# Parameters in three PSUM tiles, the second store in two halves, and two stores made one, in a batch normalisation that streams 33.6 MB

## Chip, cores, metric

One NeuronCore of a Trainium2 chip; the other cores are idle. The metric is device microseconds (us) of one execution, as a median over runs. The profiler's span is about 1.8 us shorter than the device time (81.7 against 83.5 us).

## Reference

```python
batch, channels, h, w = 32, 128, 32, 32          # x: float32
normalized = (x - running_mean[None, :, None, None]) / np.sqrt(running_var[None, :, None, None] + eps)
scaled = normalized * gamma[None, :, None, None] + beta[None, :, None, None]
return np.maximum(scaled, 0).astype(np.float32)
```

As a table x has 4096 rows (image and channel) of 1024 floats, 4 KB each. The kernel lays 16 consecutive rows into each of 128 partitions, and does this twice: t = 0 and t = 1, the first and the second half. "Row j" of a half is the j-th row of every partition: 128 x 4 KB = 512 KB.

## The kernel before

The parts that the change and the argument touch; cuts are marked with `# ...`.

```python
TILES = ((0, 0, 2), (0, 2, 4), (0, 4, 8), (0, 8, 16), (1, 0, 16))   # (half, first row, end)
LOAD_CUTS = {(1, 8)}
STORE_CUTS = {(0, 1)}
HALVES = {(1, 0), (1, 1)}
# ... all loads are issued by SP, in order: rows 0-1, 2-3, 4-7, 8-15, then 0-7 and 8-15 of half 1
    raw = params.tile([Q, 4, J], F32, name="raw")
    for k, src in enumerate((running_var, gamma, running_mean, beta)):
        nc.scalar.dma_start(out=raw[:, k, :], in_=src.rearrange("(q j) -> q j", j=J))
    # ... rep: a 0/1 matrix that spreads the 8 rows of parameters over 128 partitions
    cols = psum.tile([P, 4, J], F32, name="cols")
    for a, b in ((0, 2), (2, 3), (3, 4)):
        nc.tensor.matmul(cols[:, a:b, :]..., rep..., raw[:, a:b, :]..., start=True, stop=True)
    # ... std_t = sqrt(var + eps) on ACT; on DVE: rstd_t, scale_t, ms_t, bias_t
    with tc.manual_schedule(engines={mybir.EngineType.Activation}):
        for t, a, b, xt in tiles:
            first = a
            for j in range(a, b):
                # ... one activation for row j (two for rows in HALVES): Relu(scale * x + bias), in place
                if j + 1 == b or (t, j + 1) in STORE_CUTS:
                    nc.scalar.dma_start(
                        out=outr[t, :, first : j + 1, :], in_=xt[:, first - a : j + 1 - a, :]
                    )
                    first = j + 1
```

So there are six stores: row 0, row 1, rows 2 to 3, 4 to 7 and 8 to 15 of the first half, and the whole second half. In the profile one packet is the contiguous piece of one partition: rows 0 and 1 go out in 4 KB packets, rows 2 to 3 in 8 KB packets, the whole half in 64 KB packets.

Of the kernel before, what the change touches and what calls it, by code (L numbers as in the profile page):

```python
# [1 line left out]

# [4 lines left out]


F32 = mybir.dt.float32
ACTF = mybir.ActivationFunctionType  # L10



J = 16

TILES = ((0, 0, 2), (0, 2, 4), (0, 4, 8), (0, 8, 16), (1, 0, 16))

LOAD_CUTS = {(1, 8)}
STORE_CUTS = {(0, 1)}

HALVES = {(1, 0), (1, 1)}


@with_exitstack
def kernel(
    ctx: ExitStack,
    tc: tile.TileContext,
    x: bass.AP,
    gamma: bass.AP,
    beta: bass.AP,  # L30
    running_mean: bass.AP,
    running_var: bass.AP,
    eps: bass.AP,
    out: bass.AP,
):
    nc = tc.nc
    B, C, H, W = x.shape
    HW = H * W
    P = nc.NUM_PARTITIONS
    assert C % J == 0 and P % (C // J) == 0 and (B * C) % (P * J) == 0  # L40
    Q = C // J
    T = B * C // (P * J)

    xr = x.rearrange("b c h w -> (b c) (h w)").rearrange("(t p j) w -> t p j w", p=P, j=J)
    outr = out.rearrange("b c h w -> (b c) (h w)").rearrange("(t p j) w -> t p j w", p=P, j=J)

    data = ctx.enter_context(tc.tile_pool(name="data", bufs=1))
    params = ctx.enter_context(tc.tile_pool(name="params", bufs=1))
    psum = ctx.enter_context(tc.tile_pool(name="psum", bufs=1, space=bass.MemoryType.PSUM))

    tiles = []
    for t, a, b in TILES:
        xt = data.tile([P, b - a, HW], F32, name=f"x{t}_{a}")
        cuts = [a] + [j for j in range(a + 1, b) if (t, j) in LOAD_CUTS] + [b]
        for c, d in zip(cuts, cuts[1:]):
            nc.sync.dma_start(out=xt[:, c - a : d - a, :], in_=xr[t, :, c:d, :])  # L56
        tiles.append((t, a, b, xt))



    raw = params.tile([Q, 4, J], F32, name="raw")
    for k, src in enumerate((running_var, gamma, running_mean, beta)):
        nc.scalar.dma_start(out=raw[:, k, :], in_=src.rearrange("(q j) -> q j", j=J))
    eps_t = params.tile([P, 1], F32, name="eps_t")
    nc.vector.memset(eps_t, float(eps))  # L65
    rep = params.tile([Q, P // Q, Q], F32, name="rep")
    nc.gpsimd.memset(rep, 1.0)  # L67
    nc.gpsimd.affine_select(  # L68
        out=rep,
        in_=rep,  # L70
        compare_op=mybir.AluOpType.is_equal,
        fill=0.0,
        base=0,
        pattern=[[0, P // Q], [-1, Q]],
        channel_multiplier=1,
    )
    cols = psum.tile([P, 4, J], F32, name="cols")


    for a, b in ((0, 2), (2, 3), (3, 4)):  # L80
        nc.tensor.matmul(  # L81
            cols[:, a:b, :].rearrange("p k j -> p (k j)"),
            rep.rearrange("q r s -> q (r s)"),
            raw[:, a:b, :].rearrange("q k j -> q (k j)"),
            start=True,
            stop=True,
        )
    std_t = params.tile([P, J], F32, name="std_t")
    nc.scalar.activation(out=std_t, in_=cols[:, 0, :], func=ACTF.Sqrt, bias=eps_t[:, 0:1], scale=1.0)  # L89
    rstd_t = params.tile([P, J], F32, name="rstd_t")  # L90
    nc.vector.reciprocal(out=rstd_t, in_=std_t)  # L91
    scale_t = params.tile([P, J], F32, name="scale_t")
    nc.vector.tensor_mul(out=scale_t, in0=cols[:, 1, :], in1=rstd_t)  # L93
    ms_t = params.tile([P, J], F32, name="ms_t")
    nc.vector.tensor_mul(out=ms_t, in0=cols[:, 2, :], in1=scale_t)  # L95
    bias_t = params.tile([P, J], F32, name="bias_t")
    nc.vector.tensor_sub(out=bias_t, in0=cols[:, 3, :], in1=ms_t)  # L97

    with tc.manual_schedule(engines={mybir.EngineType.Activation}):
        for t, a, b, xt in tiles:  # L100
            first = a
            for j in range(a, b):
                step = HW // 2 if (t, j) in HALVES else HW
                for w in range(0, HW, step):
                    nc.scalar.activation(  # L105
                        out=xt[:, j - a, w : w + step],
                        in_=xt[:, j - a, w : w + step],
                        func=ACTF.Relu,
                        bias=bias_t[:, j : j + 1],
                        scale=scale_t[:, j : j + 1],  # L110
                    )
                if j + 1 == b or (t, j + 1) in STORE_CUTS:
                    nc.scalar.dma_start(
                        out=outr[t, :, first : j + 1, :], in_=xt[:, first - a : j + 1 - a, :]
                    )
                    first = j + 1


# [1 line left out]
_INS = ['x', 'gamma', 'beta', 'running_mean', 'running_var', 'eps']  # L120
_OUTS = [((32, 128, 32, 32), 'float32')]

_NUMBERS = {'eps': 1e-05}


# [26 lines left out]
```

## Time and profile before

| | before |
|---|---|
| device time | 83.57 us median of 6 (83.50 to 83.71) |
| span of the profile | 81.7 us |
| ACT busy | 39.1 us |
| loads (q1) | 48.6% of 81.7 us = 39.7 us per DMA engine |
| stores and parameters (q10) | 47.8% of 81.7 us = 39.1 us per DMA engine |

The two DMA rows are the ones to read. Multiply a queue's share by the span and you have the packet time of that queue on each of the 16 DMA engines (packet time is the time from a packet's start to its end). The prediction works with these two rows and shows the lines. The timeline says when a store is issued (start, duration, engine and line; `x2` would be two issues in one entry):

```profile
9.44 1.24 ACT L105 ACTIVATE x<-x,bias_t,scale_t 128x1024 f32<-128x1024 f32 x1 [1.02 <-DVE bias_t L97]
10.71 0.38 ACTq L113 DMA_DIRECT2D out_dram<-x  x1
...
12.41 0.37 ACTq L113 DMA_DIRECT2D out_dram<-x  x1
...
55.95 0.34 ACTq L113 DMA_DIRECT2D out_dram<-x  x1
```

The waits of SP show that its last two loads are not issued at once; each waits for an earlier transfer with which it shares a semaphore:

```profile
SPq L56 <- DMA raw<-in_running_mean_dram: 4.0, 1, 4.0
SPq L56 <- DMA x<-in_x_dram: 0.9, 1, 0.9
```

### The profile page before, as it was taken

Reading aid. Unit: us, or ns where it says so; the run is one execution under the profiler, and the core shown is the slowest. Engines: PE = TensorE matmul, PEld = TensorE weight load, DVE = VectorE, ACT = ScalarE, POOL = GpSimd, SP = SyncE. Lnnn points to the kernel's source line nnn. Section 1 sums busy time; section 2 is a strip of 40 time slices with the busy share of each in tenths; the row PEclk is TensorE's granted clock in tenths of the full one; section 3 lists DMA queues with packets and bytes.
Section 4 is the critical chain, followed back from the end, with each engine's and each line's share of the span. In section 5 each row is a group of like instructions: output and inputs, shape, how many; then the busy total and the mean of one; then the engine's idle time right before and its main releaser. Section 6 shows DMA issues by size and latency. Waiting matters only on the chain.

```text
span 81.7 us, 128 instructions
## 1 busy us (share of the span) xinstructions
PE 1.7 (2%) x6; PEld 1.5 (2%) x6; DVE 0.8 (1%) x5; ACT 39.1 (48%) x36; POOL 0.8 (1%) x6
## 2 busy tenths in 40 slices
PE   0008000000000000000000000000000000000000
PEld 0007000000000000000000000000000000000000
DVE  0000300000000000000000000000000000000000
ACT  0600477799039999199997199993000000000000
POOL 3000000000000000000000000000000000000000
DMA  2899999989899898969789699996991999998290
GB/s 44 313 422 481 409 481 417 497 369 497 369 385 481 375 491 357 541 293 605 321 373 589 273 489 393 513 497 273 513 770 64 449 513 513 513 513 385 128 513 0
DMA packets 1793, 33.56 MB, mean 411 GB/s; under 512 B 257, under 2 KB 257, under 8 KB 513
## 3 DMA queue, kind: packets, MB, share of 16 engines
q1 hardware_dynamic: 864, 16.78, 48.6%
q10 hardware_dynamic: 928, 16.78, 47.8%
q14 instruction: 1, 0.00, 0.0%
HBM read 16.78 MB, written 16.78 MB: 411 GB/s over the span
## 4 chain that ended last, share of the span: by engine, by line
DMA 56%; ACT 10%; issue 2%; SPq 0%
DMA x<-in_x_dram 56%; ACT x L105 10%; SPq L56 0%
## 5 line engine op out<-in xcount | busy, mean ns | idle before, releaser
L105 ACT ACTIVATE x<-x,bias_t,scale_t 128x1024 f32<-128x1024 f32 (+1 forms) x34 | 37.5, 1178 | 10.0 <-DMA x<-in_x_dram 7.7
L89 ACT ACT_TABLE_LOAD x1 | 1.3, 1283 | 2.7 <-issue 2.7
L89 ACT ACTIVATE std_t<-cols,eps_t 128x16 f32<-128x16 f32 x1 | 0.3, 276 | 4.2 <-PE cols L81 4.2
L81 PE MATMUL cols<-raw,rep 8*128 8x16 f32 (+1 forms) x6 | 1.7, 384 | 6.4 <-DMA raw<-in_gamma_dram 6.3
L81 PEld LDWEIGHTS cols<-raw,rep 8*128 8x128 f32 x6 | 1.5, 307 | 6.5 <-issue 6.3
L68 POOL TENSOR_SCALAR_AFFINE_SELECT rep<-rep 8x128 f32<-8x128 f32 x1 | 0.4, 394 | 0.1
L91 DVE RECIPROCAL rstd_t<-std_t 128x16 f32<-128x16 f32 x1 | 0.3, 253 | 7.5 <-ACT std_t L89 7.5
L67 POOL MEMSET rep<- 8x128 f32 x1 | 0.2, 195 | 0.3 <-POOLq L133 0.3
L93 DVE TENSOR_TENSOR scale_t<-cols,rstd_t 128x16 f32<-128x16 f32 x1 | 0.2, 174 | 0.1
L95 DVE TENSOR_TENSOR ms_t<-cols,scale_t 128x16 f32<-128x16 f32 x1 | 0.2, 174 | 0.0
L97 DVE TENSOR_TENSOR bias_t<-cols,ms_t 128x16 f32<-128x16 f32 x1 | 0.2, 174 | 0.0
L133 POOL MEMSET const-bfloat16-1.0<- 128x1 bf16 x1 | 0.1, 108 | 0.0
L133 POOL MEMSET const-float32-0.0<- 128x1 f32 x1 | 0.1, 105 | 0.3 <-issue 0.3
L133 POOL MEMSET const-uint8-127<- 128x1 uint8 x1 | 0.1, 107 | 0.0
L133 POOL MEMSET const-float32-1.0<- 128x1 f32 x1 | 0.1, 105 | 0.0
L65 DVE MEMSET eps_t<- 128x1 f32 x1 | 0.1, 59 | 0.9 <-PEq L133 0.9
## 6 DMA issues: line engine op xcount, KB each, us to landing
x<-in_x_dram SPq DMA_DIRECT2D x3, 4096.0 KB, 38.6
out_dram<-x ACTq DMA_DIRECT2D x1, 4096.0 KB, 28.6
x<-in_x_dram SPq DMA_DIRECT2D x2, 1024.0 KB, 5.8
x<-in_x_dram SPq DMA_DIRECT2D x1, 2048.0 KB, 11.3
out_dram<-x ACTq DMA_DIRECT2D x1, 2048.0 KB
out_dram<-x ACTq DMA_DIRECT2D x2, 512.0 KB, 19.1
out_dram<-x ACTq DMA_DIRECT2D x1, 1024.0 KB
raw<-in_running_var_dram ACTq DMA_DIRECT2D x1, 0.5 KB
```

The costliest lines, as they stand in the source:

```text
L65: nc.vector.memset(eps_t, float(eps))
L67: nc.gpsimd.memset(rep, 1.0)
L68: nc.gpsimd.affine_select(out=rep, in_=rep, compare_op=mybir.AluOpType.is_equal, fill=0.0, base=0, pattern=[[0, P // Q], [-1, Q]], channel ...
L81: nc.tensor.matmul(cols[:, a:b, :].rearrange("p k j -> p (k j)"), rep.rearrange("q r s -> q (r s)"), raw[:, a:b, :].rearrange("q k j -> q ...
L89: nc.scalar.activation(out=std_t, in_=cols[:, 0, :], func=ACTF.Sqrt, bias=eps_t[:, 0:1], scale=1.0)
L91: nc.vector.reciprocal(out=rstd_t, in_=std_t)
L93: nc.vector.tensor_mul(out=scale_t, in0=cols[:, 1, :], in1=rstd_t)
L95: nc.vector.tensor_mul(out=ms_t, in0=cols[:, 2, :], in1=scale_t)
L97: nc.vector.tensor_sub(out=bias_t, in0=cols[:, 3, :], in1=ms_t)
L105: nc.scalar.activation(out=xt[:, j - a, w : w + step], in_=xt[:, j - a, w : w + step], func=ACTF.Relu, bias=bias_t[:, j : j + 1], scale=sc ...
L133: nc = _bacc.Bacc("TRN2", target_bir_lowering=False, num_devices=1)
```

## The change

The intent is to start the stores sooner and to use fewer, larger packets: three PSUM tiles let the square root start when the first pair of parameters is there; row 1 is stored in two halves of 64 partitions; rows 4 to 15 leave in one store of 48 KB packets. One more row of the second half is computed in two activations.

```diff
-TILES = ((0, 0, 2), (0, 2, 4), (0, 4, 8), (0, 8, 16), (1, 0, 16))
+TILES = ((0, 0, 2), (0, 2, 4), (0, 4, 16), (1, 0, 16))
-LOAD_CUTS = {(1, 8)}
+LOAD_CUTS = {(0, 8), (1, 8)}
+TWO_PARTS = {(0, 1)}
-HALVES = {(1, 0), (1, 1)}
+HALVES = {(1, 0), (1, 1), (1, 2)}
-    raw = params.tile([Q, 4, J], F32, name="raw")
+    raw = {}
+    for a, srcs in ((0, (running_var, gamma)), (2, (running_mean,)), (3, (beta,))):
+        raw[a] = params.tile([Q, len(srcs), J], F32, name=f"raw{a}")
 ...
-    cols = psum.tile([P, 4, J], F32, name="cols")
+    cols = []
     for a, b in ((0, 2), (2, 3), (3, 4)):
+        c = psum.tile([P, b - a, J], F32, name=f"cols{a}")
 ...
                 if j + 1 == b or (t, j + 1) in STORE_CUTS:
-                    nc.scalar.dma_start(
-                        out=outr[t, :, first : j + 1, :], in_=xt[:, first - a : j + 1 - a, :]
-                    )
+                    parts = P // 2 if (t, j) in TWO_PARTS else P
+                    for p in range(0, P, parts):
+                        nc.scalar.dma_start(
+                            out=outr[t, p : p + parts, first : j + 1, :],
+                            in_=xt[p : p + parts, first - a : j + 1 - a, :],
+                        )
```

The loads are the same six as before.

More of the change, by code (lines that the diff above doesn't have):

```diff
@@ L57 @@
         tiles.append((t, a, b, xt))
-    raw = params.tile([Q, 4, J], F32, name="raw")
-    for k, src in enumerate((running_var, gamma, running_mean, beta)):
-        nc.scalar.dma_start(out=raw[:, k, :], in_=src.rearrange("(q j) -> q j", j=J))
+    raw = {}
+    for a, srcs in ((0, (running_var, gamma)), (2, (running_mean,)), (3, (beta,))):
+        raw[a] = params.tile([Q, len(srcs), J], F32, name=f"raw{a}")
+        for k, src in enumerate(srcs):
+            nc.scalar.dma_start(out=raw[a][:, k, :], in_=src.rearrange("(q j) -> q j", j=J))
     eps_t = params.tile([P, 1], F32, name="eps_t")
@@ L76 @@
     )
-    cols = psum.tile([P, 4, J], F32, name="cols")
+    cols = []
     for a, b in ((0, 2), (2, 3), (3, 4)):
+        c = psum.tile([P, b - a, J], F32, name=f"cols{a}")
         nc.tensor.matmul(
-            cols[:, a:b, :].rearrange("p k j -> p (k j)"),
+            c.rearrange("p k j -> p (k j)"),
             rep.rearrange("q r s -> q (r s)"),
-            raw[:, a:b, :].rearrange("q k j -> q (k j)"),
+            raw[a].rearrange("q k j -> q (k j)"),
             start=True,
@@ L87 @@
         )
+        cols.append(c)
     std_t = params.tile([P, J], F32, name="std_t")
-    nc.scalar.activation(out=std_t, in_=cols[:, 0, :], func=ACTF.Sqrt, bias=eps_t[:, 0:1], scale=1.0)
+    nc.scalar.activation(
+        out=std_t, in_=cols[0][:, 0, :], func=ACTF.Sqrt, bias=eps_t[:, 0:1], scale=1.0
+    )
     rstd_t = params.tile([P, J], F32, name="rstd_t")
@@ L92 @@
     scale_t = params.tile([P, J], F32, name="scale_t")
-    nc.vector.tensor_mul(out=scale_t, in0=cols[:, 1, :], in1=rstd_t)
+    nc.vector.tensor_mul(out=scale_t, in0=cols[0][:, 1, :], in1=rstd_t)
     ms_t = params.tile([P, J], F32, name="ms_t")
-    nc.vector.tensor_mul(out=ms_t, in0=cols[:, 2, :], in1=scale_t)
+    nc.vector.tensor_mul(out=ms_t, in0=cols[1][:, 0, :], in1=scale_t)
     bias_t = params.tile([P, J], F32, name="bias_t")
-    nc.vector.tensor_sub(out=bias_t, in0=cols[:, 3, :], in1=ms_t)
+    nc.vector.tensor_sub(out=bias_t, in0=cols[2][:, 0, :], in1=ms_t)
     with tc.manual_schedule(engines={mybir.EngineType.Activation}):
@@ L112 @@
                 if j + 1 == b or (t, j + 1) in STORE_CUTS:
-                    nc.scalar.dma_start(
-                        out=outr[t, :, first : j + 1, :], in_=xt[:, first - a : j + 1 - a, :]
-                    )
+                    parts = P // 2 if (t, j) in TWO_PARTS else P
[3 more added lines that the diff above has]
+                            in_=xt[p : p + parts, first - a : j + 1 - a, :],
+                        )
                     first = j + 1
```

## The prediction

> **What bounds the kernel now.** I read the page first, slice by slice. The DMA row is the mean busy share of the 16 DMA engines in tenths, the ACT row that of the only engine that computes on x.
>
> ```profile
> span 81.7 us, 128 instructions
> ...
> ACT  0600477799039999199997199993000000000000
> ...
> DMA  2899999989899898969789699996991999998290
> ```
>
> ACT is finished by slice 27 of 40 (about 56 us) and has holes before that. The DMA row stays at 8 to 9 almost throughout; the low digits near the end are large packets counted in one slice or the next, not rests. The queue list gives the proof: q1 carries the loads, q10 the stores and the four small parameter loads.
>
> ```profile
> q1 hardware_dynamic: 864, 16.78, 48.6%
> q10 hardware_dynamic: 928, 16.78, 47.8%
> HBM read 16.78 MB, written 16.78 MB: 411 GB/s over the span
> ```
>
> 48.6% + 47.8% = 96.4% of 81.7 us is 78.8 us of packet time on every engine. Only 2.9 us of the span are left. The packet records of the trace say where those lie: the first packet starts 1.8 us after the span's start, the last ends at 80.6 us, and the rest is the closing semaphores. Between the two the number of packets in flight is 16 in every microsecond. The view by windows, cut at the landings of the loads (busy time is in the first columns, DMA share and GB/s in the last two), agrees:
>
> ```profile
> 12.00:23.00 11.00, 0.00 (x0) 0.00 (x0) 0.00 (x0) 7.38 (x7) 0.00 (x0) 1.00 0.99 419
> 23.00:34.00 11.00, 0.00 (x0) 0.00 (x0) 0.00 (x0) 9.16 (x8) 0.00 (x0) 1.00 1.00 430
> 34.00:46.40 12.40, 0.00 (x0) 0.00 (x0) 0.00 (x0) 9.71 (x10) 0.00 (x0) 1.00 1.01 433
> 46.40:80.20 33.80, 0.00 (x0) 0.00 (x0) 0.00 (x0) 9.16 (x8) 0.00 (x0) 1.00 1.00 433
> ```
>
> DMA share is 0.99 to 1.01 in every stretch. The 33.80 us after the last load are stores alone, at 433 GB/s. So the kernel is bound by bytes through 16 engines, with no idle time inside. The chain that ended last names ACT and the loads, but it stops at the issue of the last store (55.95 us) and cannot see that this store then queues behind others. The waits of ACT show what the change aims at:
>
> ```profile
> ACT x L105 <- DMA x<-in_x_dram: 7.7, 3, 3.6
> ...
> ACT std_t L89 <- PE cols L81: 4.2, 1, 4.2
> ...
> ACT x L105 <- DVE bias_t L97: 1.0, 1, 1.0
> ```
>
> ACT waits 4.2 us for all of cols before the square root, and 1.0 us for the bias. These waits are on the way to the first store, not on the way to the end, as long as the loads keep the engines full meanwhile.
>
> **What the Trainium skill says.** The page "DMA: Bandwidth & Descriptors", section "Where 436 GB/s comes from", puts the ceiling at 435.2 GB/s; the 433 of the last window agrees, so the store phase has no speed to gain. The same page, "Queues, rings and completion order", says that each engine takes turns between its queues at packet granularity. The packet records agree: until the loads end, each 32 KB load packet (1.22 us) alternates with one store packet, whatever its size (4 KB 0.159 us, 8 KB 0.309 us). The same page, "Rules for kernel authors", on two transfers to disjoint partition halves: "Don't bother — they serialize"; no transfer of 64 partitions is in this trace, so it cannot confirm it. The page "PSUM — Partial Sum Buffer", section "PSUM bank collisions raise a hardware error", asks to guard PSUM by bank, not by address. That fits the trace: std_t needs only the first pair of matmuls but starts at 8.15 us, just after the sixth.
>
> **Part 1, three PSUM tiles.** Same four small transfers, same six matmul passes, same DVE instructions; only the waits move. By the trace gamma lands and PE starts at 6.3 us, the first parameter pair is in PSUM at 6.93 us, the mean at 7.48, beta at 8.11 (each held up by the landing of its parameter). Now: std_t at 8.15, reciprocal 8.45, scale 8.82, ms 9.03, bias 9.23, first ReLU at 9.44. After: std_t at about 7.0, reciprocal 7.3, scale about 7.7, ms about 7.9 (mean is there), bias waits for beta until about 8.15, first ReLU about 8.4. So about 1.05 us sooner, and the first store is issued at about 9.65 in place of 10.71 us. Until then loads alone hold all 16 engines busy (window 2 to 12 us: share 1.00), so a store that starts sooner only takes turns sooner. Gain at the end: 0.0.
>
> **Part 2, row 1 stored in two.** One more issue on ACT's queue (0.34 to 0.38 us each in the trace). The bytes and the 4 KB packets are the same, 8 per engine in all, if each half spreads over all 16 engines. ACT does idle later (3.59 us before rows 8 to 15, 2.27 us before the last eight rows), so 0.4 us there is absorbed. With part 3 the number of stores stays six. Cost: 0.0.
>
> **Part 3, rows 4 to 15 of the first half in one store.** A sum by packet size, per engine, from the packet records: eight packets of 16 KB at 0.611 us and eight of 32 KB at 1.213 us become eight of 48 KB. 64 KB takes 2.418, so doubling 32 KB saves 2 x 1.213 - 2.418 = 0.008 us and doubling 16 KB saves 0.009. Estimate for 48 KB: 0.611 + 1.213 - 0.008 = 1.816 us. Saved: 8 x 0.008 = 0.07 us. That is all the change removes from the bounding engines.
>
> The danger is in when this store is issued: at about 33 us instead of 20.27 for its first third. But the store queue serves in order, and with one store packet per load packet it is busy with rows 0 to 3 for very long: these are 24 packets per engine, and the loads of rows 8 to 15 and of the second half are also 24. In the trace rows 2 and 3 finish only at 46.7 us, when the loads (46.4 us) are just done. So the 16 KB packets that could have started at 20 us started at 46.4 us, and the late store still has 13 us to spare. With part 1 the small stores finish perhaps 1 us sooner, which leaves 12.
>
> **Part 4, row 2 of the second half in two halves.** Two activations of 0.80 us in place of one of 1.23: +0.37 us on ACT, before a hole of 2.27 us. Cost: 0.0.
>
> **The end.** After the loads, the stores of rows 4 to 15 and of the whole second half are left: 14.7 MB, 33.9 us at 433 GB/s. The last store (rows 0 to 15 of the second half) must be issued before the queue runs dry. Now: last load lands at 46.7, eight activations take 9.16 us, issue at 55.95; the store before it ends at 61.2 us. Margin 5 us, less one or two for the way from issue to first packet. After: about 0.2 us more store packets come between the loads, so issue at about 56.2 us, and the 48 KB packets end at about 61. The margin holds.
>
> Sum: 83.55 - 0.07 + 0.0 = 83.48 us.
>
> **Rivals.**
> (a) The earlier start is passed on to the end: 83.55 - 1.05 = 82.5 us. This would need engines that idle for lack of stores. Against it: 16 packets in flight in every microsecond from 2 to 80. I give it 2%.
> (b) A half of 64 partitions is served badly (fewer engines, or two engines pulling from the same part of SBUF). For it: the form is new here. Estimate: if its 8 packets of 0.159 us per engine took twice as long, 1.3 us if it all fell on the sum, 84.8 us; more likely only part, 83.7 to 84.2. About 8%.
> (c) A new wait at the issue of a store. Transfers share a few semaphores, and some wait for an earlier transfer to land before they are issued (SP waits 4.0 us for a parameter in front of a load of x). If the last store came to wait for the store just before it (61 us), the engines would run dry: about 1 us of wait after the last packet and some 1.5 to 3.9 us to the first packet of the new one, 85.5 to 88 us. Against it: there are sixteen transfers before and after, and the last one's partner was the store of row 0, landed long before. 2%.
> (d) The pair of 64-partition stores, or the shifted turns, put the engines out of step so that one ends later. Now the 16 engines end within 0.34 us of each other; a few tenths at most.
>
> **Range and chances.** The three runs before lie within 0.12 us. Below, nothing but 0.07 us and startup scatter (the first 8 KB load packets average 0.344 us against 0.309, so 16 x 0.035 = 0.6 us per engine is the most that luck could give). Above, (b) and (d). Range 83.2 to 83.9 us. Faster by over 2% needs 1.7 us out of 2.9 us of idle span, which the change doesn't touch: 1%. Slower by over 2% needs (c): 2%.
>
> **What would show it.** Right: first ReLU near 8.4 us; q1 and q10 again about 96% together, with the same bytes and some 128 fewer packets; 48 KB packets of about 1.82 us beginning when the loads end, near 46.5 us; the last store issued near 56 us; DMA share 1.00 in each window; the span at 81.6 us. Wrong: a window after 46 us with a share under 0.97 (rival c); 4 KB store packets well over 0.16 us (rival b); or a first packet or last landing that moved by more than 0.3 us.

## The result

| | before | after |
|---|---|---|
| device time, median of 6 | 83.57 us | 83.53 us |
| range | 83.50 to 83.71 | 83.44 to 83.74 |
| span of the profile | 81.7 us | 81.7 us |
| first ReLU / first store issued | 9.44 / 10.71 us | 8.33 / 9.60 us |
| last load has landed / last store issued | 46.7 / 55.95 us | 46.8 / 56.05 us |

The ratio is 0.9996 (95% interval 0.9981 to 1.001). Ratios here are the mean of one kernel's runs over the mean of the other's in the same rounds, so they are not quite the ratios of the medians quoted beside them. Executions over 1.5% slower than the fastest of the same kernel are left out of the means.

The page of the kernel after, the span and the queues:

```profile
span 81.7 us, 129 instructions
...
q1 hardware_dynamic: 864, 16.78, 48.6%
q10 hardware_dynamic: 800, 16.78, 47.7%
```

128 packets fewer on q10, and 0.1% of the span (0.08 us) less packet time. Its windows, cut as the prediction cut those of before:

```profile
12.00:23.00 11.00, 0.00 (x0) 0.00 (x0) 0.00 (x0) 7.00 (x6) 0.00 (x0) 1.00 0.99 418
23.00:34.00 11.00, 0.00 (x0) 0.00 (x0) 0.00 (x0) 9.16 (x8) 0.00 (x0) 1.00 1.00 427
34.00:46.40 12.40, 0.00 (x0) 0.00 (x0) 0.00 (x0) 9.99 (x11) 0.00 (x0) 1.00 1.03 441
46.40:80.20 33.80, 0.00 (x0) 0.00 (x0) 0.00 (x0) 9.16 (x8) 0.00 (x0) 1.00 0.99 430
```

The share (the number before the last) is as full as before. The waits of ACT moved as intended, 4.2 to 2.7 us for PSUM:

```profile
ACT std_t L95 <- PE cols L86: 2.7, 1, 2.7
```

The timeline shows the start 1.1 us sooner and, at 11.30, the two issues of row 1, which take 1.18 us where the one issue took 0.37; the last store is not sooner:

```profile
8.33 1.24 ACT L113 ACTIVATE x<-x,bias_t,scale_t 128x1024 f32<-128x1024 f32 x1 [1.46 <-DVE bias_t L105]
9.60 0.39 ACTq L123 DMA_DIRECT2D out_dram<-x  x1
...
11.30 1.18 ACTq L123 DMA_DIRECT2D out_dram<-x  x2
...
56.05 0.34 ACTq L123 DMA_DIRECT2D out_dram<-x  x1
```

One thing was not foreseen: the semaphores are shared out differently, and the last load is now issued at 12.77 us instead of 8.11, since SP waits for rows 4 to 7 to land:

```profile
SPq L58 <- DMA x<-in_x_dram: 5.0, 1, 5.0
```

It costs nothing, because the data of that load do not move before 34 us in either kernel.

### The profile page after: what moved, and what is told of

The parts are those of the page before. It is cut to its first block, busy times and chain, and to the rows that moved or that the text cites. A ratio compares the mean times of both kernels' runs of the same rounds, so it can differ in the third digit from the quotient of the medians.

```text
span 81.7 us, 129 instructions
## 1 busy us (share of the span) xinstructions
PE 1.8 (2%) x6; PEld 1.5 (2%) x6; DVE 0.8 (1%) x5; ACT 39.3 (48%) x37; POOL 0.8 (1%) x6
## 4 chain that ended last, share of the span: by engine, by line
DMA 55%; ACT 10%; issue 2%; SPq 1%
DMA x<-in_x_dram 55%; ACT x L113 10%; SPq L58 1%
```

## The experiments

All agree with the reference. Each ran beside the kernel before on the same chip. The medians of before in the three sets were 83.54 us (first four runs), 83.55 (next four) and 83.49 (last four).

The first theory was that of the prediction: the engines are always full, only the sum of packet times counts, each part is worth about nothing. The rival was that two effects cancel.

### Undo part 1: one raw tile, one cols tile

```diff
-    raw = {} ...; c = psum.tile([P, b - a, J], ...) per pair
+    raw = params.tile([Q, 4, J], F32, name="raw"); cols = psum.tile([P, 4, J], F32, name="cols")
```

> The changed kernel with part 1 undone: one raw tile and one cols tile again. First theory (engines always full, an earlier first store only takes turns earlier): first ReLU back at about 9.4 us, time 83.5 us, ratio to the kernel before 0.998 to 1.002. Rival (two effects cancel: the earlier start gives about 1 us and another part takes it away): about 84.5 us, ratio about 1.012.

Measured: 83.92 us, ratio 1.0046 (1.0031 to 1.0061). It lies between the two: too slow for the first theory, and not slow enough for the rival.

### Undo part 2: row 1 in one store

```diff
-TWO_PARTS = {(0, 1)}
+TWO_PARTS = set()
```

> The changed kernel with row 1 stored in one transfer of 128 partitions. First theory: nothing at the end, 83.5 us, although ACT starts row 2 about 0.8 us sooner. Rival (the 64-partition pair costs what the earlier start gives): 82.5 us, ratio 0.988.

Measured: 84.34 us, ratio 1.0095 (1.0082 to 1.0109). Both were wrong: without the pair of halves the kernel is slower by 0.8 us, although ACT starts row 2 sooner.

### Undo part 3: rows 4 to 7 and 8 to 15 stored separately

```diff
-STORE_CUTS = {(0, 1)}
+STORE_CUTS = {(0, 1), (0, 8)}
```

> The changed kernel with rows 4 to 7 and 8 to 15 stored separately again, in packets of 16 and 32 KB. First theory: eight packets of 48 KB (1.815 us) become eight of 16 KB (0.611) and eight of 32 KB (1.213), 0.07 us more per engine: 83.6 us, too little to be told from noise. The sum of packet times in the trace should be 0.07 us higher per engine. Rival (the late issue of the joined store costs, hidden by the gain of the earlier start): 82.5 to 83.0 us.

Measured: 83.77 us, ratio 1.003 (1.0015 to 1.0045). The packet records give 14.59 us per engine for rows 4 to 15 instead of 14.52, the 0.07 us of the theory; the rest of the 0.23 us is not in the stores. The interval lies above that of the changed kernel (0.9981 to 1.001), so the difference is not noise alone. Its runs spread from 83.64 to 84.05, and the profiled one was the 84.05.

### All stores in two halves of 64 partitions

```diff
-                    parts = P // 2 if (t, j) in TWO_PARTS else P
+                    parts = P // 2
```

> Every store of x in two transfers of 64 partitions each, also the large ones. First theory (each half spreads over all 16 engines, four packets on each, at the same time per packet): 83.5 us, packets of 64 KB still at 2.418 us. Rival (64 partitions are served by fewer engines, or two engines pull from the same part of SBUF at half the rate): the 33.8 us of stores after the loads take up to twice as long, so anything from 90 to 115 us.

Measured: 116.81 us, ratio 1.398. The rival holds for the large stores. Two windows of this run, both stores alone (the last three numbers are clock, DMA share, GB/s):

```profile
46.80:60.00 13.20, 0.00 (x0) 0.00 (x0) 0.00 (x0) 8.90 (x8) 0.00 (x0) 1.00 1.00 233
60.00:74.00 14.00, 0.00 (x0) 0.00 (x0) 0.00 (x0) 0.00 (x0) 0.00 (x0) 1.00 1.03 229
```

The share is 1.0, and the rate is 233 GB/s where the kernel after has 430. A full DMA row says that packets are in flight, not that they are fast: 64 KB packets took 4.68 us on average here, 2.418 before. The 4 KB packets, which take turns with loads, still took 0.159 us. So the form leaves the packet time as it was where the change uses it, and nearly doubles it for a store that has the engines to itself. Fewer engines are not the reason: 15 to 17 packets were in flight at every microsecond from 47 to 110 us. That two engines pull from the same part of SBUF fits this, but no run shows it.

### The start made 6 and 20 us later

```diff
+    # ... idle_t: an unused tile of 128 x 1024, set to 0 by GpSimd
+        for _ in range(5):        # 16 in the second run
+            nc.scalar.activation(out=idle_t, in_=idle_t, func=ACTF.Relu, ...)
         for t, a, b, xt in tiles:
```

> The changed kernel with five activations on an unused tile in front of the first ReLU, which starts 5.7 us later (5 x 1.13). First theory (the start of the stores has slack, since loads fill the engines and the small stores only take turns): 83.5 us. Rival (the first store's time is passed on to the end): 89 us.

> The same with sixteen unused activations: first ReLU about 18.1 us later, at 26.4. ACT then never waits for a load any more: rows 0 to 15 done at about 47, the last store issued at about 65.9 us in place of 56.05. The loads end about 42.5 us, the store queue runs dry once near 47 (about 2 us) and again before the last store (about 4 us). First theory: the slack is used up and the time grows by about 6 us, to 89.6 us (87 to 92). If the slack were unlimited: 83.5; if every microsecond counted: 101.6.

Measured: 84.23 us (ratio 1.0081) and 92.20 us (1.1031). An unused activation takes 1.27 us (20.34 / 16), not 1.13; the rows of x take 1.145 (9.16 / 8). That each waits for the one before it, since all work in place on one tile, would explain this, but is not shown. The first ReLU was 6.5 and 20.4 us later. Of 6.5 us, 0.7 us reached the end, so the slack is real but not free. Of 20.4 us, 8.7 us did. The windows of the second run show where: the engines ran dry twice, once for 3.3 us and once for 4.1 us.

```profile
46.90:50.20 3.30, 0.00 (x0) 0.00 (x0) 0.00 (x0) 2.88 (x4) 0.00 (x0) 1.00 0.01 5
...
65.60:69.70 4.10, 0.00 (x0) 0.00 (x0) 0.00 (x0) 3.31 (x3) 0.00 (x0) 1.00 0.00 0
```

The last store left at 68.94 us; I had expected 65.9 and 89.6 us in all. The longer activations explain most of the miss.

### Rows 0 to 3 in one store of 16 KB packets

```diff
-TILES = ((0, 0, 2), (0, 2, 4), (0, 4, 16), (1, 0, 16))
+TILES = ((0, 0, 4), (0, 4, 16), (1, 0, 16))
-LOAD_CUTS = {(0, 8), (1, 8)};  STORE_CUTS = {(0, 1)};  TWO_PARTS = {(0, 1)}
+LOAD_CUTS = {(0, 2), (0, 8), (1, 8)};  STORE_CUTS = set();  TWO_PARTS = set()
```

> Rows 0 to 3 of the first half stored in one transfer, 16 KB packets, 8 per engine in place of 24 small ones. Same bytes, fewer and larger packets, so the sum of packet times is slightly lower. First theory (one store packet per load packet, whatever its size): the store of rows 4 to 15, issued near 34 us, then takes turns with the last loads, eight times 1.82 + 1.22 us, so the last load lands at about 60 us in place of 46.8, the last store is issued about 70 us, the engines run dry for about 10 us, time about 94 us (90 to 96). Rival (only the sum of packet times counts, the order of the stores is free): 83.5 us.

Measured: 93.79 us; of four runs one took 99.65 us and is left out of the ratio, 1.1212. As expected from turns of one packet each, large store packets now stood between the last loads. ACT's waits and a window of this run:

```profile
ACT x L113 <- DMA x<-in_x_dram: 23.6, 3, 12.7
```

```profile
62.50:71.00 8.50, 0.00 (x0) 0.00 (x0) 0.00 (x0) 7.68 (x7) 0.00 (x0) 1.00 0.00 0
```

ACT waited 12.7 us for the last load, and the DMA engines then stood still for 8.5 us for want of a store. Fewer and larger packets cost 10 us. The 24 small store packets per engine in the two kernels are what lets the 24 large load packets through.

### All stores from row 2 on in 8 KB packets

```diff
-STORE_CUTS = {(0, 1)}
+STORE_CUTS = {(0, 1)} | {(t, j) for t in (0, 1) for j in range(2, 16, 2)}
```

> All stores from row 2 on in pieces of two rows, 8 KB packets. First theory (the time is fixed cost plus the sum of packet times): 15 pieces x 8 x 0.309 + 16 x 0.159 = 39.6 us of store packets per engine in place of 38.9, so 0.75 us more: 84.3 us, unless a piece has to wait for an earlier one to land and the queue runs dry. Rival (the size of packets does not matter): 83.5 us.

Measured: 84.80 us, ratio 1.0138 (1.0107 to 1.017). The packet records give 39.63 us for the stores, as worked out (0.75 us more). The other 0.5 us are not in the stores: in the profiled run the loads took 0.2 us longer than in the kernel after (39.9 against 39.7 us per engine), and the engines' last packets ended 1.16 us apart instead of 0.43.

### Reading the turns

Four of these runs (part 1 undone, part 2 undone, 6 us later, 8 KB packets) were 0.4 to 0.8 us slower than the sum of the stores allows. The packet records show it. They do not name the engine, so I chained them: each packet follows the one that ended when it started, in sixteen chains. Where several packets end within nanoseconds of each other a chain can cross to another engine, so the counts below are surer than any single chain. Below is the commonest chain of each kernel, from the first 32 KB load on; L is a load packet of 32 KB, 4 and 8 are store packets of 4 and 8 KB, and | is where the large stores begin.

```
before      LL4L4L4L4L4L4L44LL4L4L4L4L4L4L44LL8L8L8L8L8L8L88|
after       L4L4L4L4L4L4L4L4L4L4L4L4LL4L4L44LL8L8L8L8L8L8L88|
undo part 1 LL4L4L4L4L4L4L44LL4L4L4L4LL4L44L4LL8L8L8L8L8L888|
undo part 2 L4L4L4L4L4L4L4L4L4L4L4L4L4L4L4L4L8L8L8L8L8L8L8L8|
6 us later  LLLLLLL4L44L4L4L4L4L4LL4L44L4LL4L4L4L4LL88888888|
```

Two loads in a row (LL) are a turn that the store queue missed; mostly this happens where one store ends and the next begins. Part 1 lets the stores enter one load sooner. Part 2 adds a boundary, and with it one missed turn. Together they leave the stores where they were: in the kernels before and after, every engine has just two small packets left when its last load ends. Undo one part and it is three, or one.

That was the second theory: **parts 1 and 2 offset each other through the phase of the turns**, and a phase other than that of before costs 0.3 to 0.8 us. Four runs tested it, and all four came out within the ranges given in advance.

### Part 1 alone and part 2 alone, on the kernel before

The edits are the hunks for raw and cols, and the hunk with `TWO_PARTS`, of the diff above.

> The kernel before with part 1 alone (three raw and three cols tiles). New theory (parts 1 and 2 offset each other: what counts is how many small store packets each engine has left when its last load ends; 2 on every engine in the kernels before and after): first ReLU about 8.4 us, first store packet one load packet sooner, so 1 packet left, engines out of step, about 84.2 us (83.8 to 84.5). First theory (engines are full, nothing counts but the sum of packets): 83.55 us.

> The kernel before with part 2 alone (row 1 stored in two halves). New theory: the additional boundary between two stores costs the store queue one turn, so 3 small packets are left at the end of the loads, the last load packet is longer (about 1.5 us in place of 1.22) and the time about 83.9 us (83.7 to 84.1). First theory: 83.55 us.

Measured: 84.16 us (ratio 1.0078, 1.0065 to 1.0091) and 83.98 us (1.0065, 1.0052 to 1.0078), with one packet left (none to two) and three (two to four). Each part alone makes the kernel slower; both together do not.

### One unused activation, with and without the halves

```diff
+        for _ in range(1):
+            nc.scalar.activation(out=idle_t, in_=idle_t, func=ACTF.Relu, ...)
         for t, a, b, xt in tiles:
```

The first run has it in the kernel with part 2 undone, the second in the changed kernel.

> The changed kernel with row 1 in one store (84.34 us when it ran alone) and one unused activation in front of the first ReLU, which moves the first store 1.13 us later, back to where the kernel before has it. New theory (only the phase of the turns counts, not the form with 64 partitions): 2 packets left on every engine, 83.5 us (83.4 to 83.7), faster than without the additional work. Rival (the 64-partition form itself brings the gain): still 84.3 us. Rival (additional work on ACT costs something): 84.3 or more.

> The changed kernel with one unused activation in front of the first ReLU, the first store 1.13 us later. New theory: one turn later, 3 packets left, like the run with part 1 undone: 83.9 us (83.7 to 84.1). First theory: 83.5 us.

Measured: 83.57 us median (six runs: four from 83.49 to 83.59, one 83.80, one 84.45; ratio 1.0035, 1.0003 to 1.0067) and 83.83 us (1.0047, 1.0035 to 1.0059). **The same additional work, 1.1 us before the first store, takes 0.77 us off one kernel (84.34 to 83.57) and adds 0.30 us to the other (83.53 to 83.83).** These are medians from different sets; by the ratios to the kernel before it is about 0.5 us off (1.0095 to 1.0035, with its two slower runs counted) and 0.4 us on (0.9996 to 1.0047). The first has two packets left on every engine in its profile, the second three (four on two engines). So neither the form with 64 partitions nor an earlier start is good or bad in itself here; the phase is what counts. Two of the six runs of the first were slower all the same, so the good phase is not held safely.

Where the time sits can be read from the queue lines. In order: part 1 alone, part 2 alone, part 2 undone, part 2 undone plus one activation. These are profiled runs; the table below gives their own device times beside the medians.

```profile
span 82.4 us, 129 instructions
...
q1 hardware_dynamic: 864, 16.78, 48.8%
q10 hardware_dynamic: 928, 16.78, 47.4%
```

```profile
span 82.5 us, 128 instructions
...
q1 hardware_dynamic: 864, 16.78, 48.6%
q10 hardware_dynamic: 944, 16.78, 47.3%
```

```profile
span 82.5 us, 128 instructions
...
q1 hardware_dynamic: 864, 16.78, 48.9%
q10 hardware_dynamic: 784, 16.78, 47.2%
```

```profile
span 81.7 us, 131 instructions
...
q1 hardware_dynamic: 864, 16.78, 48.6%
q10 hardware_dynamic: 784, 16.78, 47.7%
```

Share times span: the loads took 40.2, 40.1, 40.3 and 39.7 us per engine, the stores 39.1, 39.0, 38.9 and 39.0. The stores are the same and the loads, of the same bytes, are longer in the slow phases. The records put much of it on the last load packet of each engine, and the rest of the loss is that the engines no longer finish together:

| kernel | small packets left | mean of the last load packet | engines' last ends lie within | profiled run | median |
|---|---|---|---|---|---|
| before | 2 | 1.245 us | 0.34 us | 83.44 us | 83.49 to 83.57 us |
| after | 2 | 1.213 | 0.43 | 83.45 | 83.53 |
| part 2 undone, one activation | 2 | 1.274 | 0.43 | 83.49 | 83.57 |
| part 3 undone | 1 to 4 | 1.303 | 0.74 | 84.05 | 83.77 |
| changed, one activation | 3 to 4 | 1.618 | 0.59 | 84.03 | 83.83 |
| part 1 undone | 3 | 1.519 | 0.50 | 83.87 | 83.92 |
| part 2 alone | 2 to 4 | 1.537 | 0.65 | 84.26 | 83.98 |
| part 1 alone | 0 to 2 | 1.648 | 0.54 | 84.15 | 84.16 |
| part 2 undone | 0 to 2 | 1.664 | 0.95 | 84.43 | 84.34 |
| 6 us later | 7 to 9 | 1.857 | 0.69 | 84.31 | 84.23 |

With part 3 undone, parts 1 and 2 are both in place, yet its slow profiled run has only about half of the engines at two packets; its six runs spread over 0.41 us. So the two parts do not offset each other in every run.

A rival is when SP issues the last load, which also changes from run to run. It does not go with the time: it is 8.04 to 8.19 us in the kernel before, with part 1 alone, with part 2 undone and in both runs with one activation, and 12.77 to 12.95 us in the kernel after, with part 1 undone, with part 2 alone and with part 3 undone. Fast and slow kernels stand on both sides.

The count of packets left marks the phase; why the last load packet grows from 1.21 to 1.5 or 1.9 us in the other phases is open. The run with 16 KB packets first has none left on any engine and a last load of 1.213 us, so the count itself is not the cause.

## Why the prediction was right or wrong

The number was right: 83.5 predicted, 83.53 measured, with the interval of the ratio on both sides of 1. The steps:

- **The bound.** Right. Loads and stores fill the engines in both kernels, and the run that was 20 us late shows what it costs when they don't. But "the number of packets in flight is 16 in every microsecond" was taken as proof that nothing can change, and that is too much. The slower kernels also have 16 in flight until their last microsecond or so; their packets take longer. Likewise the stores in halves, with a share of 1.0 at 233 GB/s.
- **Part 1, "Gain at the end: 0.0".** The mechanism (sooner, and only turns change) was right: 8.33 us against about 8.4. The size was wrong: alone it costs 0.67 us (84.16 against 83.49), because the shifted turns lengthen the loads (40.2 against 39.7 us per engine) and spread the engines' ends. The prediction lets each 32 KB load packet alternate with one store packet until the loads end; the chains show turns that a queue missed (LL and 44), and these are what parts 1 and 2 move.
- **Part 2, "Cost: 0.0".** Wrong as well: alone it costs 0.49 us (83.98 against 83.49). ACT's own cost was mis-sized too: the second issue added 0.8 us (1.18 against 0.37), not 0.34 to 0.38, but ACT's later wait for a load (3.90 us) absorbed it, as argued. The two costs cancel in the sum by luck: the two shifts offset each other, which the prediction did not see. Its rival (d) named the shifted turns, and "a few tenths at most" was too small for 0.3 to 0.8 us.
- **Part 3.** 48 KB packets took 1.815 us (1.816 estimated) and started at 46.3 us (46.5 expected). The 0.07 us of packet time is there. Undoing the part cost 0.23 us, more than that; in the one profiled run, the slowest of six, the engines ended 0.74 us apart, and why is open. The argument that the late store is protected by the 24 small packets is shown by the run that took them away: 93.79 us.
- **Part 4** was not tested by itself. In the profile after, ACT still idles 2.15 us before the last eight rows, as argued.
- **Rivals.** (a) did not happen: 1.1 us of earlier start gave nothing, and 6.5 us of later start cost 0.7. (b) did not happen in the change, where the halves travel among loads; for stores alone it is real, 1.9 times the packet time. (c) did not happen to a store; the one new wait is SP's, and it is harmless. Its 1.5 to 3.9 us from the issue to the first packet was too long: the last store of the run that was 20 us late, which found the engines idle, took 0.84 us (68.94 to 69.78).

No version faster than both was found. In the kernel after, 78.7 of the 80.6 us up to the last packet are packet time, and 1.8 us come before the first packet.

## What to carry to other kernels

In this kernel, bound by DMA bytes, an earlier start of the stores bought nothing. In one like it, ask instead which queue's packets stand between the last loads, and keep the early stores in small packets so that the loads get through. A change that measures "same" may be two changes of 0.5 to 0.7 us that offset each other, so run each part alone, and where turns are shared, shift the phase by an idle instruction before crediting or blaming the edit. A full DMA row is time, not bytes: read GB/s beside it.

## What the Trainium skill lacked or had wrong

- "DMA: Bandwidth & Descriptors", section "Rules for kernel authors", says of two transfers to disjoint partition halves that they serialize and aren't worth it. Large stores bear this out: 116.81 us against 83.54 us. The row names no exception for small stores among loads: there 4 KB packets of such halves were not slower than those of whole rows (0.159 us).
- The same page, section "Queues, rings and completion order", gives a turn as a packet of typically about 9 to 17 descriptors. In these traces a turn is one record of the profile, a contiguous piece of one partition, from 4 to 48 KB (the traces do not count descriptors), so a queue with larger pieces takes a larger share: 93.79 us when a store of 48 KB pieces took turns with 32 KB loads.
- No page has the phase effect: with the same bytes in the loads, load time per engine went from 39.7 us to between 40.0 and 40.4 us and device time up by 0.3 to 0.8 us, by a shift of the first store (about 1 us, and 6.5 us in one run) or by one boundary between stores.
